# S5 loop of a hybrid S5 and Hyena encoder block: input matrices on VectorE, the skip's diagonal prepared once and added on GpSimd

## The chip, the core and the metric

The kernel runs on one core of a Trainium2 chip. The metric is the device time of one execution in microseconds (us), the median of several runs. Engines are named as in the profile: PE is TensorE (matmuls), PEld its weight loads, DVE is VectorE, ACT is ScalarE, POOL is GpSimd, SP issues DMAs.

## What is computed

One encoder block over 1024 positions of width 1024. Its first half merges two token mixers, a bidirectional S5 state-space model and an order-2 Hyena convolution; its second half is a SwiGLU channel mixer. The change concerns the S5 mixer alone:

```python
def _s5_scan(u, lam_re, lam_im, log_step, b_re, b_im, c_re, c_im, reverse):
    # abar = exp(lam * step), bb = (abar - 1) / lam * b, all complex
    ug = u.reshape(bsz, seq, S5_GROUPS, S5_GROUP)            # 32 groups of 16 channels
    bu_re = jnp.einsum('blgc,gpc->lbgp', ug, bb_re)          # 64 states a group
    bu_im = jnp.einsum('blgc,gpc->lbgp', ug, bb_im)
    # s[l] = abar * s[l-1] + bu[l], along the sequence or against it
    return (jnp.einsum('lbgp,gcp->blgc', s_re, c_re) - jnp.einsum('lbgp,gcp->blgc', s_im, c_im)).reshape(bsz, seq, D_S5)

def _s5_branch(u, ...):
    y = u * d                                                # the skip, d per channel
    for direction in range(2):
        y = y + _s5_scan(u, ..., reverse=(direction == 1))
    z = gelu(y)
    return z * sigmoid(z @ glu_w + glu_b)
```

## The kernel before

The kernel is written in a tile framework. The program names tiles and instructions; a scheduler puts each engine's instructions in a fixed order by its own estimate of times and adds the waits. So the order on an engine is not that of the source, and a change in one place can move rows elsewhere. Each engine works through its own list in order.

The S5 mixer (`emit_s5`) cuts the sequence into 128 blocks of 8 positions. In each block of 8 the effect of inputs on outputs is a small local kernel; from block to block the state is carried by a scan of 128 steps. A loop `for q in range(8)` (line 779) makes four channel groups a turn; below, "group" means one turn of this loop. The two directions lie in partitions 0 to 63 (`f`) and 64 to 127 (`b`). One turn does this:

- Output matrices: `ct`, `nct` are the transposed C and its negative; `cc0`, `cc1` are C times powers of abar, four products (line 800) and two sums (line 801) on VectorE.
- Input matrices: `Bw` is B times powers of abar (`eb`), by the helper `cmul` (lines 591 and 592: four products `wt`, two sums `bw`), on GpSimd. TensorE transposes them (`tt`, line 809), ScalarE copies them into `BT`.
- Local kernel: TensorE multiplies `cc` by B (`bz`) into `kp` (line 821); ScalarE copies it to SBUF as `Kt`, and its backward half at lag 0 as `kb` (lines 825, 826). VectorE adds the skip, `diag` times the column `dcol` of d (line 827), and writes the sum at lag 0 into `Kt` (line 828). `Kt` goes to DRAM (`klines`) and comes back as the Toeplitz blocks `D` (line 834).
- Phases and rotation: lines 841 to 852 make `cos` and `sin` (two VectorE instructions over the tile, four over its quarters, `sin`); `bu` (line 859) is the input times `BT` on TensorE; lines 863 to 865 rotate it into `xs` on VectorE.
- Scan on VectorE (line 871) into `S`, rotation back: `z` on VectorE (lines 876, 877, 879), the imaginary part on GpSimd into `beside` (the same three lines). ScalarE copies both into `M`.
- Output: `yp` on TensorE, `cc` times `M` (line 885) plus `D` times the input (line 887); ScalarE copies it, DMA stores it in `zS`.

The input's projection matmuls (`pj`, lines 144 to 146, three for one product since weights `wh`, `wl` and inputs are split in two parts) for Hyena and the gates don't depend on S5 and are put between the S5 matmuls by the scheduler. Their weights are split on ScalarE (`wh`) and GpSimd (`wl`, line 136). After the loop the GLU (`emit_glu`) reads `zS` back (`zf`, line 1267) and multiplies it by its weights (`gl`).

Of the kernel before, what the change touches and what calls it, by code (L numbers as in the profile page):

```python
# [7 lines left out]
F32 = mybir.dt.float32  # L8
# [3 lines left out]
ALU = mybir.AluOpType  # L12
# [4 lines left out]
P = 128  # L17
# [566 lines left out]
def cmul(E, pool, out, a, b, shape, tag, eng=None, conj=False):  # L584

    eng = eng or E.nc.vector
    for k, op in enumerate((ALU.add, ALU.subtract) if conj else (ALU.subtract, ALU.add)):
        t = [pool.tile(shape, F32, tag=f"{tag}{i}", name=f"{tag}{i}") for i in range(2)]
        pairs = ((a[0], b[0]), (a[1], b[1])) if k == 0 else ((a[1], b[0]), (a[0], b[1]))
        for i in range(2):  # L590
            eng.tensor_tensor(out=t[i], in0=pairs[i][0], in1=pairs[i][1], op=ALU.mult)
        eng.tensor_tensor(out=out[k], in0=t[0], in1=t[1], op=op)
# [151 lines left out]
def emit_s5(E, before):  # L744
# [3 lines left out]
    V, GP = nc.vector, nc.gpsimd  # L748
    f, b = slice(0, 64), slice(64, 128)
    with ExitStack() as ctx:  # L750
        op = ctx.enter_context(E.tc.tile_pool(name="s5k", bufs=1, reuse_waits="tile"))
# [6 lines left out]
        with E.tc.tile_pool(name="s5p", bufs=1, reuse_waits="tile") as pp:  # L758
            bball, r8, wh, wl, ec, eb = s5_params(E, op, pp, ps)
            before()  # L760
        sp = ctx.enter_context(E.tc.tile_pool(name="s5", bufs=1, reuse_waits="tile"))
        halfpi = op.tile([P, 1], F32, name="halfpi")
        V.memset(halfpi, float(np.pi / 2))
        dcol = op.tile([64, 8], F32, name="dcol")
        nc.sync.dma_start(out=dcol, in_=d["s5_d"][0].rearrange("(q r) -> r q", r=64))
        diag = op.tile([64, 16], F32, name="diag")
        V.tensor_copy(diag, E.ident[0:64, 0:16])
        for g in range(1, 4):
            V.tensor_tensor(out=diag, in0=diag, in1=E.ident[0:64, 16 * g:16 * g + 16], op=ALU.add)
        bz = [op.tile([P, 640], F32, name=f"bz{k}") for k in range(2)]  # L770
        W = P + 2
        xs = [op.tile([P, 4, W], F32, name=f"xs{k}") for k in range(2)]
# [5 lines left out]
        for q in range(8):  # L778
# [6 lines left out]
            e4 = lambda ap, n, m: ap[:, :, gs].rearrange("p t g -> p g t").unsqueeze(3).to_broadcast([P, 4, n, m])  # L785
            b4 = lambda ap, n, m: ap.unsqueeze(2).to_broadcast([P, 4, n, m])
# [14 lines left out]
                V.tensor_tensor(out=CC[k], in0=tmp[0], in1=tmp[1], op=sgn)  # L801
            Bb = [x[:, gs] for x in bball]
            Bw = [T(f"bw{i}", [P, 4, 8, 16]) for i in range(2)]
            cmul(E, sp, Bw, [b4(x, 8, 16) for x in Bb], [e4(x, 8, 16) for x in eb], [P, 4, 8, 16], "wt", GP)
            BT = []
            for i in range(2):
                pt = ps.tile([P, 4, P], F32, tag="tt", name="tt", bufs=2)
# [10 lines left out]
            kp = ps.tile([P, 9, 16], F32, tag="tt", name="kp", bufs=2)  # L818
# [4 lines left out]
            Kt = T("Kt", [P, 9, 16])  # L823
            kb = T("kb", [64, 16])
            nc.scalar.copy(Kt, kp)
            nc.scalar.copy(kb, kp[b, 0])
            V.scalar_tensor_tensor(out=kb, in0=diag, scalar=dcol[:, q:q + 1], in1=kb, op0=ALU.mult, op1=ALU.add)
            V.tensor_tensor(out=Kt[f, 0], in0=kp[f, 0], in1=kb, op=ALU.add)
            line = E.klines[gs].rearrange("g c x -> (g c) x")
            nc.sync.dma_start(out=line[:, 112:240], in_=Kt[f, 0:8].rearrange("p i c -> p (i c)"))  # L830
            nc.sync.dma_start(out=line[:, 0:112], in_=Kt[b, 2:9].rearrange("p i c -> p (i c)"))
# [12 lines left out]
            for g in range(4):  # L844
                V.scalar_tensor_tensor(out=ph[:, g], in0=j8[:, 0], scalar=col(wl, 4 * q + g), in1=ph[:, g],
                                       op0=ALU.mult, op1=ALU.subtract)
# [22 lines left out]
            for i in range(2):  # L869
                o, r, x = fl(S[i]), fl(rd), fl(xs[i])  # L870
                V.tensor_tensor_scan(out=o[:, 1:n], data0=r[:, 0:n - 1], data1=x[:, 0:n - 1], initial=0.0,
                                     op0=ALU.mult, op1=ALU.add)
# [911 lines left out]
def hybrid_block(tc, d):  # L1784
# [4 lines left out]
    with ExitStack() as top:  # L1789
# [18 lines left out]
        with ExitStack() as s0:  # L1808
            E.h0 = pool(s0, "h0")
            E.dft = pool(s1, "dft")  # L1810
            with ExitStack() as s2:
# [25 lines left out]
                for ct in range(4):  # L1837
                    emit_conv(E, ct)
                emit_ada(E, (2, 4, 3), *ada_rooms(E))
                emit_s5(E, lambda: [emit_u(E, ct) for ct in range(4)])  # L1840
                for ct in range(4, 12):
                    emit_conv(E, ct)
# [70 lines left out]
```

## Time and profile before

| | |
|---|---|
| median of 3 runs | 1740.43 us (1737.8 to 1741.24) |
| profiled execution | 1738.77 us, its span 1737.0 us |
| TensorE matmuls busy | 1552.6 us, 89% of the span |
| VectorE busy | 1326.7 us, 76% |
| ScalarE busy | 744.1 us, 43% |
| GpSimd busy | 641.1 us, 37% |

The S5 loop runs from about 393 to 630 us of the span. Shares over the whole span are averages over stages with different limits; what a change in one stage is worth is read from that stage, by what ended each engine's idle time there. The starts of one instruction in successive turns of a loop give the time of a turn, and the duration of the same instruction with and without work on another engine shows what the two do to each other.

### The profile page before, as it was taken

The numbers are of one execution on the slowest core, as the hardware profiler recorded it, in microseconds if no ns is written. First come the engines' busy times: TensorE is split into PE (matmuls) and PEld (weight loads), VectorE is DVE, ScalarE is ACT, GpSimd is POOL, SyncE is SP. The second block draws the span as 40 slices with busy tenths as digits, with TensorE's granted clock in tenths as the row PEclk, the third lists the DMA queues.
The fourth block names the chain that finished last, engine by engine and source line by source line (L and its number), as shares of the span: only waits on it lengthen the run. The fifth ranks groups of instructions, "written<-read, shape, count | busy, mean of one in ns | idle before, by whom it ended". The sixth has DMA issues, their size and how long they took to land. (4 is left out here: it accounts for less than half of the span.)

```text
span 1737.0 us, 22072 instructions
## 1 busy us (share of the span) xinstructions
PE 1552.6 (89%) x7598; PEld 1282.6 (74%) x7598; DVE 1326.7 (76%) x1927; ACT 744.1 (43%) x1366; POOL 641.1 (37%) x425
## 2 busy tenths in 40 slices
PE   6778889997678798998869999899999999999996
PEld 2666768785556686786757989688888888878884
DVE  6889798787898835788877656976676777579976
ACT  5846455443453444412223455533333333345445
POOL 3356564326575426768862121111111111012233
PEclk9998999998897999999989999899999999999998
DMA  9446643432122344864425853143323223499953
GB/s 329 123 141 185 181 132 113 153 100 82 50 71 67 88 112 156 285 233 155 122 85 184 279 181 97 49 135 113 104 92 103 92 97 99 146 380 319 328 190 126
DMA packets 244870, 263.81 MB, mean 152 GB/s; under 512 B 27672, under 2 KB 168816, under 8 KB 243317
## 3 DMA queue, kind: packets, MB, share of 16 engines
q1 hardware_dynamic: 244278, 259.99, 46.8%
q0 software_dynamic: 480, 2.42, 0.4%
q8 instruction: 60, 0.98, 0.2%
q14 instruction: 52, 0.43, 0.1%
HBM read 195.00 MB, written 67.34 MB: 151 GB/s over the span
## 5 line engine op out<-in xcount | busy, mean ns | idle before, releaser
L144 PE MATMUL pj<-hT,wh 128*128 128x512 f32 x480 | 195.6, 407 | 8.7 <-ACT cva L1184 8.0
L136 POOL TENSOR_TENSOR wl<-wf,wh 128x1024 fp32r<-128x1024 f32 (+1 forms) x56 | 127.9, 2285 | 200.3 <-ACT wh L135 150.1
L146 PE MATMUL pj<-hT,wl 128*128 128x512 f32 x480 | 194.8, 406 | 4.6 <-POOL wl L136 4.6
L136 POOL TENSOR_TENSOR wl<-wg,wh 128x1024 fp32r<-128x1024 f32 x22 | 55.4, 2521 | 345.3 <-ACT wh L135 345.3
L146 PE MATMUL gu<-h2T,op 128*128 128x512 f32 x440 | 172.8, 394 | 3.8 <-DVE op L136 3.8
L144 PE MATMUL gu<-h2T,op 128*128 128x512 f32 x440 | 171.4, 394 | 2.5 <-ACT op L135 2.5
L145 PE MATMUL gu<-h2T,op 128*128 128x512 f32 x440 | 173.1, 393 | 0.0
L135 ACT CAST op<-ws 128x512 fp32r<-128x512 f32 x88 | 54.4, 622 | 182.9 <-PE gu L146 111.1
L145 PE MATMUL dn<-dop 128*128 128x512 f32 x308 | 120.2, 390 | 0.3 <-POOL dop L136 0.3
L146 PE MATMUL dn<-dop 128*128 128x512 f32 x308 | 120.0, 390 | 0.0
L144 PEld LDWEIGHTS pj<-hT,wh 128*128 128x128 f32 x480 | 94.6, 197 | 28.3 <-ACT cva L1184 8.7
L144 PE MATMUL dn<-dop 128*128 128x512 f32 x308 | 112.3, 391 | 2.2 <-ACT dop L135 2.1
L146 PEld LDWEIGHTS pj<-hT,wl 128*128 128x128 f32 x480 | 94.3, 196 | 25.1 <-POOL wl L136 5.4
L145 PE MATMUL pj<-hT,wh 128*128 128x512 f32 x256 | 102.9, 402 | 0.0
L146 PEld LDWEIGHTS gu<-h2T,op 128*128 128x128 f32 x440 | 83.6, 190 | 22.4 <-DVE op L136 5.0
L144 PEld LDWEIGHTS gu<-h2T,op 128*128 128x128 f32 x440 | 83.5, 190 | 21.5 <-ACT op L135 3.2
L145 PEld LDWEIGHTS gu<-h2T,op 128*128 128x128 f32 x440 | 83.5, 190 | 17.0
L145 PE MATMUL pj<-lT,wh 128*128 128x512 f32 x224 | 91.1, 407 | 0.0
L136 POOL TENSOR_TENSOR dop<-bf,dop 128x512 fp32r<-128x512 f32 x17 | 31.4, 1852 | 128.7 <-ACT dop L135 112.6
L1535 DVE TENSOR_TENSOR ws<-wu 128x512 f32<-128x512 f32 x22 | 25.3, 1149 | 64.0 <-DMA wu<-in_ffn_w_gu_dram 64.0
L144 PE MATMUL wop<-woh,mT 128*128 128x256 f32 x256 | 73.1, 286 | 0.9 <-DVE tmp L1410 0.9
L135 ACT CAST wh<-wf 128x1024 fp32r<-128x1024 f32 (+1 forms) x56 | 50.0, 893 | 55.5 <-PE pj L145 24.6
(461 smaller groups left out, 4494.0 us busy)
## 6 DMA issues: line engine op xcount, KB each, us to landing
bf<-in_ffn_w_down_dram SPq DMA_DIRECT2D x105, 256.0 KB
wf<-in_w_in_dram SPq DMA_DIRECT2D x36, 512.0 KB
ada<-in_ada_w_dram SPq DMA_DIRECT2D x48, 256.0 KB
wg<-in_ffn_w_gu_dram SPq DMA_DIRECT2D x22, 512.0 KB
wu<-in_ffn_w_gu_dram SPq DMA_DIRECT2D x22, 512.0 KB
adS<-S SPq DMA_DIRECT2D x44, 256.0 KB
af<-adS SPq DMA_DIRECT2D x44, 256.0 KB
adA<-a SPq DMA_DIRECT2D x33, 256.0 KB
```

The costliest lines, as they stand in the source:

```text
L135: E.nc.scalar.copy(hi, src)
L136: (lo_eng or E.nc.vector).tensor_tensor(out=lo, in0=src, in1=bc(hi), op=ALU.subtract)
L144: E.nc.tensor.matmul(out=out, lhsT=lh, rhs=rh, start=first, stop=False, skip_group_check=shared)
L145: E.nc.tensor.matmul(out=out, lhsT=lh, rhs=rl, start=False, stop=False, skip_group_check=shared)
L146: E.nc.tensor.matmul(out=out, lhsT=ll, rhs=rh, start=False, stop=last, skip_group_check=shared)
L1535: V.tensor_tensor(out=s1, in0=u1, in1=u2, op=ALU.add)
```

## The change

The six instructions of `cmul` for `Bw` go from GpSimd to VectorE (48 in the loop). The diagonal matrices of the skip, `dd`, are made once ahead of the loop, by eight small VectorE instructions; inside it GpSimd adds `dd[:, q]` to `kb` and then `kb` to `Kt` at lag 0. VectorE no longer touches the local kernel, and line 828 no longer reads `kp` from PSUM, which GpSimd adds to from `Kt` instead.

```diff
--- before.py
+++ after.py
@@ -767,6 +767,9 @@
         V.tensor_copy(diag, E.ident[0:64, 0:16])
         for g in range(1, 4):
             V.tensor_tensor(out=diag, in0=diag, in1=E.ident[0:64, 16 * g:16 * g + 16], op=ALU.add)
+        dd = op.tile([64, 8, 16], F32, name="dd")
+        for q in range(8):
+            V.tensor_scalar(out=dd[:, q], in0=diag, scalar1=dcol[:, q:q + 1], scalar2=None, op0=ALU.mult)
         bz = [op.tile([P, 640], F32, name=f"bz{k}") for k in range(2)]
         W = P + 2
         xs = [op.tile([P, 4, W], F32, name=f"xs{k}") for k in range(2)]
@@ -801,7 +804,7 @@
                 V.tensor_tensor(out=CC[k], in0=tmp[0], in1=tmp[1], op=sgn)
             Bb = [x[:, gs] for x in bball]
             Bw = [T(f"bw{i}", [P, 4, 8, 16]) for i in range(2)]
-            cmul(E, sp, Bw, [b4(x, 8, 16) for x in Bb], [e4(x, 8, 16) for x in eb], [P, 4, 8, 16], "wt", GP)
+            cmul(E, sp, Bw, [b4(x, 8, 16) for x in Bb], [e4(x, 8, 16) for x in eb], [P, 4, 8, 16], "wt")
             BT = []
             for i in range(2):
                 pt = ps.tile([P, 4, P], F32, tag="tt", name="tt", bufs=2)
@@ -824,8 +827,8 @@
             kb = T("kb", [64, 16])
             nc.scalar.copy(Kt, kp)
             nc.scalar.copy(kb, kp[b, 0])
-            V.scalar_tensor_tensor(out=kb, in0=diag, scalar=dcol[:, q:q + 1], in1=kb, op0=ALU.mult, op1=ALU.add)
-            V.tensor_tensor(out=Kt[f, 0], in0=kp[f, 0], in1=kb, op=ALU.add)
+            GP.tensor_tensor(out=kb, in0=kb, in1=dd[:, q], op=ALU.add)
+            GP.tensor_tensor(out=Kt[f, 0], in0=Kt[f, 0], in1=kb, op=ALU.add)
             line = E.klines[gs].rearrange("g c x -> (g c) x")
             nc.sync.dma_start(out=line[:, 112:240], in_=Kt[f, 0:8].rearrange("p i c -> p (i c)"))
             nc.sync.dma_start(out=line[:, 0:112], in_=Kt[b, 2:9].rearrange("p i c -> p (i c)"))
```

The scheduler orders the whole program anew. Lines behind the new ones count three higher in the listings of the new kernel.

VectorE, between the first sum `cc0` of a group and the rotation of `bu`, in the third group, before (the number behind a tile's name is its buffer):

```order
L801 TENSOR_TENSOR cc0_3188<-rt0_3190,rt1_3191 128x576
L843 SCALAR_TENSOR_TENSOR ph_3425<-phk_3426,ph_3425 128x512
L800 TENSOR_TENSOR rt0_3195<-nct_3185,ec1_2486 128x576
L800 TENSOR_TENSOR rt1_3196<-nct_3185,ec0_2485 128x576
L845 SCALAR_TENSOR_TENSOR ph_3425<-j8_2291,s5keep_2529,ph_3425 128x128 x4
L801 TENSOR_TENSOR cc1_3189<-rt0_3195,rt1_3196 128x576
L863 TENSOR_TENSOR rt0_3297<-bu0_3279,cos_3260 128x512
L827 SCALAR_TENSOR_TENSOR kb_3240<-diag_2825,dcol_2823,kb_3240 64x16
L864 TENSOR_TENSOR rt1_3298<-bu1_3288,sin_3261 128x512
```

The same place in the fourth group, after:

```order
L804 TENSOR_TENSOR cc0_3364<-rt0_3366,rt1_3367 128x576
L591 TENSOR_TENSOR wt0_3550<-bb1_2512,eb0_2487 128x512
L591 TENSOR_TENSOR wt1_3551<-bb0_2511,eb1_2488 128x512
L845 TENSOR_SCALAR phk_3602<-ph_3601 128x512
L803 TENSOR_TENSOR rt0_3371<-nct_3361,ec1_2486 128x576
L803 TENSOR_TENSOR rt1_3372<-nct_3361,ec0_2485 128x576
L592 TENSOR_TENSOR bw1_3544<-wt0_3550,wt1_3551 128x512
L846 SCALAR_TENSOR_TENSOR ph_3601<-phk_3602,ph_3601 128x512
L804 TENSOR_TENSOR cc1_3365<-rt0_3371,rt1_3372 128x576
L591 TENSOR_TENSOR wt0_3712<-bb0_2511,eb0_2487 128x512
L591 TENSOR_TENSOR wt1_3713<-bb1_2512,eb1_2488 128x512
L848 SCALAR_TENSOR_TENSOR ph_3601<-j8_2291,s5keep_2529,ph_3601 128x128 x4
```

In the one, the local kernel's line 827 stands between the two uses of `bu`; in the other it is gone, and five instructions of `cmul` stand between `cc0` and the first use of `bu`, of the next group's input matrices and the one after.

GpSimd in the loop, from a weight split on, before:

```order
L136 TENSOR_TENSOR wl_5020<-wf_5017,wh_5019 128x1024
L876 TENSOR_TENSOR beside_2840<-S0_2973,sin_2927 128x512
L592 TENSOR_TENSOR bw0_3200<-wt0_3202,wt1_3203 128x512
L877 TENSOR_TENSOR beside_2840<-S1_2974,cos_2926 128x512
L591 TENSOR_TENSOR wt0_3207<-bb1_2512,eb0_2487 128x512
L591 TENSOR_TENSOR wt1_3208<-bb0_2511,eb1_2488 128x512
L879 TENSOR_TENSOR beside_2840<-beside_2840 128x512
L592 TENSOR_TENSOR bw1_3201<-wt0_3207,wt1_3208 128x512
L591 TENSOR_TENSOR wt0_3369<-bb0_2511,eb0_2487 128x512
```

and after, again from a weight split on:

```order
L136 TENSOR_TENSOR wl_5089<-wf_5086,wh_5088 128x1024
L830 TENSOR_TENSOR kb_3082<-kb_3082,dd_2830 64x16
L879 TENSOR_TENSOR beside_2849<-S0_3149,sin_3103 128x512
L831 TENSOR_TENSOR Kt_3081<-Kt_3081,kb_3082 64x16
L880 TENSOR_TENSOR beside_2849<-S1_3150,cos_3102 128x512
L882 TENSOR_TENSOR beside_2849<-beside_2849 128x512
L136 TENSOR_TENSOR wl_5149<-wf_5146,wh_5148 128x1024
L879 TENSOR_TENSOR beside_2849<-S0_3316,sin_3270 128x512
L830 TENSOR_TENSOR kb_3249<-kb_3249,dd_2830 64x16
```

The input matrices have left; the two adds of the local kernel stand among the products `beside` of the same group: in the second group the second add behind the first product, in the third (the last two rows) both behind it. That is so for one add or both in four of eight groups; in the others both adds stand ahead of the products.

On TensorE the order changes in which projection matmuls stand where. Behind the last `yp` and ahead of the first GLU matmul there are 162 of them before and 123 after; the loop, from its first transpose to its last `yp`, holds 413 before and 441 after. Before the loop's first transpose 11 more run after the change than before it. All or most of `bu` stands behind the last `kp` of its group in the fourth, the sixth and the eighth group after the change, and a part of it behind the first `kp` in the second. In the FFN some rows of VectorE, ScalarE and TensorE change places; nothing is added or removed there.

## Rows read from the trace of the kernel before

**Rows 1.** Busy time by stretch (start:end us, length), with granted TensorE clock.

```profile
core 0: us, PE busy (x) PEld busy (x) DVE busy (x) ACT busy (x) POOL busy (x), PEclk, DMA share, GB/s
392.90:630.20 237.30, 185.65 (x1070) 151.87 (x1071) 196.90 (x206) 100.76 (x217) 131.47 (x79) 0.86 0.26 71
630.20:673.00 42.80, 38.21 (x168) 30.95 (x167) 8.94 (x4) 22.59 (x23) 14.61 (x6) 1.00 0.55 151
```

**Rows 2.** What TensorE waited for, 392.9 to 630.2 us: total, times, longest.

```profile
PE kp L821 <- DVE cc L801: 33.6, 8, 7.2
PE yp L885 <- ACT M L881: 16.0, 7, 3.6
```

**Rows 3.** What VectorE waited for, the same stretch.

```profile
DVE kb L827 <- ACT kb L826: 23.4, 4, 6.2
```

**Rows 4.** Line 879 on VectorE: min/median/max ns, first and last start.

```profile
L879 DVE TENSOR_TENSOR z<-rt,rt x8: 673/1478/2765, 434.4 to 620.1; 128x512 f32<-128x512 f32 x8
```

**Rows 5.** Timeline of VectorE, last group: start us, us, instruction [idle before].

```profile
600.59 2.77 DVE L879 TENSOR_TENSOR z<-rt,rt 128x512 f32<-128x512 f32 x1
...
604.95 1.41 DVE L800 TENSOR_TENSOR rt<-ct,ec 128x576 f32<-128x576 f32 x2
...
617.33 1.67 DVE L877 TENSOR_TENSOR rt<-S,sin 128x512 f32<-128x512 f32 x1
...
620.11 0.67 DVE L879 TENSOR_TENSOR z<-rt,rt 128x512 f32<-128x512 f32 x1
```

**Rows 6.** Timeline of VectorE in an earlier group.

```profile
493.02 3.24 DVE L800 TENSOR_TENSOR rt<-ct,ec 128x576 f32<-128x576 f32 x2
...
498.10 3.05 DVE L800 TENSOR_TENSOR rt<-nct,ec 128x576 f32<-128x576 f32 x2
```

**Rows 7.** Timeline of GpSimd in the same stretch.

```profile
492.51 3.13 POOL L591 TENSOR_TENSOR wt<-bb,eb 128x512 f32<-128x512 f32 x2
```

**Rows 8.** Timeline of VectorE: a product of `cmul`, and the steps of a phase.

```profile
370.87 0.68 DVE L591 TENSOR_TENSOR bt<-braw,s5scr 128x512 f32<-128x512 f32 x1
...
444.62 0.41 DVE L842 TENSOR_SCALAR phk<-ph 128x512 f32<-128x512 f32 x1
...
445.63 0.68 DVE L843 SCALAR_TENSOR_TENSOR ph<-phk,ph 128x512 f32<-128x512 f32 x1
...
447.43 1.12 DVE L845 SCALAR_TENSOR_TENSOR ph<-j,s5keep,ph 128x128 f32<-128x128 f32 x4
```

**Rows 9.** Timeline of VectorE, first group.

```profile
390.31 0.41 DVE L842 TENSOR_SCALAR phk<-ph 128x512 f32<-128x512 f32 x1
...
414.90 0.76 DVE L801 TENSOR_TENSOR cc<-rt,rt 128x576 f32<-128x576 f32 x1
...
422.16 0.23 DVE L827 SCALAR_TENSOR_TENSOR kb<-diag,dcol,kb 64x16 f32<-64x16 f32 x1 [5.70 <-ACT kb L826]
```

**Rows 10.** Timeline of TensorE and VectorE at a wait for line 826.

```profile
477.78 0.66 PE L859 MATMUL bu<-U,BT 128*64 128x128 f32 x8
...
478.67 0.23 DVE L827 SCALAR_TENSOR_TENSOR kb<-diag,dcol,kb 64x16 f32<-64x16 f32 x1 [5.57 <-ACT kb L826]
...
478.82 0.67 DVE L864 TENSOR_TENSOR rt<-bu,sin 128x512 f32<-128x512 f32 x1
```

**Rows 11.** Timeline of TensorE: two projection matmuls, one behind the other.

```profile
480.83 0.39 PE L145 MATMUL pj<-lT,wh 128*128 128x512 f32 x1
...
481.06 0.39 PE L146 MATMUL pj<-hT,wl 128*128 128x512 f32 x1
```

**Rows 12.** Timeline of the DMA queue: line 1267 first and last, line 765.

```profile
631.37 4.32 SPq L1267 DMA_DIRECT2D zf<-zS  x6
...
653.66 1.52 SPq L1267 DMA_DIRECT2D zf<-zS  x3
...
353.01 2.17 SPq L765 DMA_DIRECT2D dcol<-in_s_d_dram  x1
```

**Rows 13.** Line 740 on GpSimd, small copies: min/median/max ns.

```profile
L740 POOL COPY s5keep<-s5scr x3: 212/215/537, 361.8 to 368.7; 128x32 f32<-128x32 f32 x3
```

## The prediction

> **What bounds the kernel now.** The change lies in the S5 loop of eight channel groups, so I read the busy time of that stretch first, then what each engine waited for in it, then the timeline of single groups.
>
> From the first matmul of the loop to its last TensorE is busy 185.65 of 237.30 us at a granted clock of 0.86, VectorE 196.90, GpSimd 131.47 [rows 1]. Right behind it the clock is 1.00 and TensorE hardly pauses [rows 1]. The time to win is therefore inside the loop, 51.65 us of TensorE's pauses at most, plus what the lower clock costs. TensorE's pauses are mainly waits for VectorE: 33.6 us before the local kernel's matmuls (`kp`, line 821) for the products `cc` (line 801), and 16.0 us before `yp` for `M`, which ScalarE copies from VectorE's `z` [rows 2]. VectorE itself waits 23.4 us in four groups for `kb`, ScalarE's copy of `kp` [rows 3]. So the loop is a circle: VectorE makes `cc`, TensorE makes `kp` and `bu`, VectorE goes on with `bu` to `z`, TensorE goes on with `z`.
>
> The beat of the circle is the start of `z` on VectorE: 434.4 us for the first, 600.59 for the seventh, 620.11 for the last [rows 4, 5]. That is (600.59 - 434.4) / 6 = 27.7 us a group for six groups, and 19.52 for the last.
>
> Why are they so different? In the last group GpSimd has no input matrices left to make, VectorE has no phase of a next group to make, and it never waits for `kb`. How much GpSimd's products matter is seen at line 800: two products take 1.41 us on VectorE in the last group [rows 5], but 3.24 and 3.05 us in an earlier one [rows 6], while GpSimd makes its own two products there in 3.13 us [rows 7]. The two engines take turns; (3.24 - 1.41) / 2 = 0.9 us is lost on VectorE for each such GpSimd instruction that meets it.
>
> **The change part by part.** The sum is made on the profiled execution (1738.77 us, span 1737.0, 1.77 us around it). That run lies 1.66 us, 0.1%, under the median of 1740.43 us; I take the difference that I find off the median.
>
> *1. Input matrices on VectorE.* 48 instructions (six a group) leave GpSimd. The same helper, the same shape, made on VectorE before the loop, takes 0.68 us [rows 8], so six cost 4.1 us a group. What a group costs without GpSimd's products I take from the last group, which is a measurement of just that: 19.52 us. It holds the remaining GpSimd work already, a weight split beside its first `z` (2.77 us against 0.67 us bare) and the `beside` products (1.67 us against 0.67 us in one instruction) [rows 5]. It lacks the phase of a next group, 0.41 + 0.68 + 1.12 = 2.2 us [rows 8]. Together 19.5 + 2.2 + 4.1 = 25.8 us, before waits, against 27.7 us with them.
>
> *2. The skip on GpSimd.* Lines 827 and 828 leave VectorE. Their work is small, 0.23 us for the first where nothing disturbs it [rows 10], so 0.2 us a group go: 25.6 us. The wait for `kb` goes too, but that is worth little by itself: at 478.67 us VectorE starts line 827 after 5.57 us of waiting, and the eight `bu` matmuls that its next instruction needs end on TensorE at 477.78 + 0.66 = 478.44 us [rows 10]. Without line 827, line 864 would have waited for `bu` until then. What counts is whether TensorE still puts `bu` behind `kp`. By the new order it does so in four of eight groups (all or most of it in the fourth, sixth and eighth, part of it in the second); but in the second, fourth and sixth VectorE now has three to five instructions of `cmul`, 2.0 to 3.4 us, to make between `cc` and `bu`, in the place of the wait. The four waits were 23.4 us, 5.70 of them in the first group [rows 3, 9], so 17.7 / 6 = 2.95 us per interval. I keep 0.4 us of it, between 0 and 2.95. An interval is then 26.0 us, and six save 6 x 1.7 = 10 us. Bounds: 25.0 us (a saving of 16; the products at 0.6, no wait) and 28.5 us (a loss of 5; the whole wait comes back).
>
> *3. The first group.* From the phase at 390.31 us to the end of the second `cc` at 415.66 VectorE takes 25.35 us [rows 9]. At the bare prices it has two phases (4.4), a sine product (0.7), and two sets of `cc` products at 1.41 + 0.76 (4.3): 9.4 us [rows 5, 8, 9]. Now come twelve products (8.2) and two meetings with weight splits of 2.1 us each, (2.77 - 0.67) [rows 5]: 21.8 us, 3.5 less. Of the wait of 5.70 us behind it [rows 9] I let the half go. Together 6 us; between 1 and 11.
>
> *4. The adds on GpSimd.* 16 small adds; small copies there take 0.21 to 0.54 us [rows 13], so 3.4 to 8.6 us in all on an engine that loses 48 instructions in the same stretch. The first of each pair waits for ScalarE's copy of `kb`; behind it stand the `beside` products or the next weight split, for which TensorE's `yp` and projections wait. GpSimd's idle time, 237.30 - 131.47 us before [rows 1], hides both; where it doesn't, it is the third rival.
>
> *5. The last group.* In the new order 3 projection matmuls stand between the last `yp` products, 19 in the order before. Two such start 0.23 us apart [rows 11], so 16 x 0.23 = 3.7 us. The last local kernel is also written earlier, ahead of the `beside` products instead of behind them. Against it stands that the eighth group's `bu` comes behind `kp` with nothing between, so that VectorE may wait there as it did not before. I take 2 us, between -3 and 4.
>
> *6. The tail.* After the last `yp` 123 projection matmuls stand in front of the GLU's, 162 before: 39 x 0.23 = 9 us, which now fill pauses of the loop. Against it stands the reload of S5's output: 32 transfers whose issue takes from 631.37 to 655.18 us [rows 12]. The remaining 123 x 0.23 = 28 us cover that with little to spare, so I give 1.5 us back: 7.5 us, between 3 and 9.
>
> *7. `dd`.* Eight VectorE instructions among the S5 parameters, on whose chain the loop begins. The like tile takes 0.23 us [rows 10]: 1.8 us. They need `dcol`, whose transfer is issued from 353.01 to 355.18 us [rows 12], about when VectorE would get to them, so it can also stand there for a moment, with all parameters behind it. I charge 2 us, between 0 and 4.5.
>
> Sum: -10 - 6 - 2 - 7.5 + 2 = -23.5 us. Later stages keep their work; a shuffle of some rows in the FFN I price at nothing, because TensorE runs on there through other rows.
>
> **The rivals.**
>
> *No gain in the loop.* VectorE gives back exactly what it wins, and `bu` takes the place of `kb`. For it: 19.5 + 2.2 + 4.1 - 0.2 + 2.95 = 28.6 us, which is no better than 27.7. Against it: the products stand where VectorE waited. With intervals of 27.7 us and nothing in the first group, the last group, the tail and `dd` are left: -2 - 7.5 + 2 = -7.5, so 1733 us. The Trainium skill, page Perfetto Trace Analysis, section Optimizing Scalar/DVE Operations, speaks for this rival: it warns that VectorE and GpSimd share a read port of SBUF, so that moving work between these two might not help. This trace agrees that they block each other (0.9 us an instruction, above); by that rule items 1 to 3 are worth nothing, and the sum is the -7.5.
>
> *Slower: the products stand ahead of `cc`.* In the new order up to five products lie between `z` and the second `cc`. TensorE's wait for `cc` [rows 2] then grows, `kp` and `bu` come later, and VectorE waits for `bu` longer than it did for `kb`. The other items are worth 13.5 us, so it decides from 13.5 / 6 = 2.3 us more per interval, 30.0 us. With a full wait of 6 us in every group, the longest of before [rows 3], an interval is 25.6 + 6 = 31.6 us: 6 x 3.9 - 13.5 = +10, so 1750 us.
>
> *GpSimd's queue.* In four groups the second of the adds, in two of them both, stand behind a `beside` product that needs the scan, so the local kernel and its reload come late and `yp` waits for `D`. Nothing waits for `D` now to speak of. At 4 us in each of four groups: -23.5 + 16 = -7.5, 1733 us.
>
> *More.* With fewer pauses the clock stays up and intervals fall to 24 us: 6 x 2 more, so -35.5, 1705 us.
>
> **How the numbers follow.** The forecast, 1707 to 1728 us around 1717, gets 0.50; no gain in the loop 0.20; slower 0.14; GpSimd's queue 0.08; more 0.08. The range runs from 1698 (into the last case) to 1740 us, which leaves out most of the slower case and a little of "more". 0.2%, 3.5 us, is about what a measurement of this kernel can tell from no change: most of the slower case lies above 1744, 0.12; between lie its rest and the upper part of "no gain", 0.10; faster is 0.78.
>
> **What would show it.** Right: starts of `z` some 26 us apart; line 800 at 0.7 to 0.8 us an instruction except beside `wl` and `beside`; little VectorE waiting, for `bu`; TensorE's wait for `cc` under 33.6 us; the first GLU matmul about 24 us earlier. Wrong: starts of `z` 28 us or more apart, with VectorE waiting for `bu` as long as it did for `kb`, or TensorE waiting for `D`.

## The result and the profile after

| | before | after |
|---|---|---|
| median | 1740.84 us (1737.8 to 1743.99, 4 runs) | 1694.97 us (1693.18 to 1695.76, 4 runs) |
| profiled execution, its span | 1738.77, 1737.0 us | 1695.38, 1693.6 us |
| first matmul of the loop | 393.01 us | 393.69 us |
| first start of `z` | 434.40 us | 421.11 us |
| mean of six intervals between starts of `z` | 27.70 us | 23.95 us |
| last interval | 19.52 us | 22.80 us |
| end of the last `yp` | 630.22 us | 594.98 us |
| first GLU matmul | 672.01 us | 623.84 us |

The ratio is 0.9738 (95% interval 0.9724 to 0.9751): 45.9 us less, where 23.5 were forecast. The sign and the place were right, the size was not: 1694.97 us lies 3 us under the low end of the range.

The busy time by stretch in the kernel after: the loop, what follows it up to the GLU, both together, and the six intervals. Columns as in [rows 1].

```profile
core 0: us, PE busy (x) PEld busy (x) DVE busy (x) ACT busy (x) POOL busy (x), PEclk, DMA share, GB/s
393.69:594.98 201.29, 178.79 (x1099) 148.57 (x1099) 182.83 (x237) 99.93 (x217) 72.27 (x50) 0.96 0.30 84
594.98:623.84 28.86, 28.34 (x124) 22.77 (x123) 7.36 (x4) 20.32 (x19) 11.16 (x5) 1.00 0.69 190
393.69:623.84 230.15, 207.13 (x1222) 171.34 (x1221) 190.19 (x241) 120.25 (x236) 83.43 (x54) 0.96 0.35 97
421.11:564.82 143.71, 126.78 (x790) 105.01 (x788) 138.12 (x179) 76.68 (x170) 53.94 (x37) 0.95 0.30 84
```

VectorE has 237 instructions in the loop instead of 206 and is nevertheless busy for 182.83 us instead of 196.90 [rows 1]. It now works through 138.12 of the 143.71 us of the six intervals; 0.93 us an interval are pauses. The granted clock of the loop is 0.96 of 2.4 GHz, 0.86 before; both are means over stretches at 2.4 GHz and stretches at 1.2 GHz.

The same two stretches of the kernel before, joined, and its six intervals (columns as above):

```profile
393.01:672.01 279.00, 222.87 (x1231) 181.96 (x1232) 205.73 (x210) 122.37 (x238) 145.70 (x84) 0.88 0.30 83
434.40:600.59 166.19, 127.39 (x740) 104.67 (x741) 146.39 (x157) 76.49 (x168) 95.40 (x57) 0.85 0.24 65
```

From the loop's first matmul to the GLU the time fell from 279.00 to 230.15 us. TensorE's busy time in it fell by 15.74 us at nearly the same number of matmuls (1231 and 1222 recorded), TensorE's pauses from 56.13 to 23.02 us.

TensorE's waits for `M` and `cc`, and VectorE's longest waits, in the loop after (us in total, times, longest):

```profile
PE yp L888 <- ACT M L884: 13.3, 7, 4.3
PE kp L824 <- DVE cc L804: 3.0, 3, 1.5
```

```profile
DVE rt L866 <- PE bu L862: 6.5, 2, 6.1
DVE bw L592 <- PE tt L812: 3.7, 2, 3.0
```

TensorE's wait for `cc`, 33.6 us [rows 2], is 3.0 us; VectorE's wait for `kb`, 23.4 us [rows 3], is gone, and `bu` takes 6.5 us in its place, nearly all of it in one wait of the last group. The wait of `yp` for `M` has hardly changed (16.0 and 13.3 us).

The groups of VectorE's instructions in the S5 stage (from 385 to 640 us), count, busy us, mean ns, before:

```profile
L800 DVE TENSOR_TENSOR rt<-ct,ec 128x576 f32<-128x576 f32 x16 | 25.8, 1649 | 0.0
L801 DVE TENSOR_TENSOR cc<-rt,rt 128x576 f32<-128x576 f32 x16 | 18.4, 1152 | 0.5
L877 DVE TENSOR_TENSOR rt<-S,sin 128x512 f32<-128x512 f32 x8 | 12.4, 1552 | 0.0
L863 DVE TENSOR_TENSOR rt<-bu,cos 128x512 f32<-128x512 f32 x16 | 11.0, 687 | 0.6
```

and after:

```profile
L591 DVE TENSOR_TENSOR wt<-bb,eb 128x512 f32<-128x512 f32 x32 | 22.7, 749 | 0.0
L592 DVE TENSOR_TENSOR bw<-wt,wt 128x512 f32<-128x512 f32 x16 | 15.6, 973 | 3.8 <-PE tt L812 3.7
L880 DVE TENSOR_TENSOR rt<-S,sin 128x512 f32<-128x512 f32 x8 | 12.5, 1566 | 0.0
L804 DVE TENSOR_TENSOR cc<-rt,rt 128x576 f32<-128x576 f32 x16 | 12.0, 752 | 0.3
L803 DVE TENSOR_TENSOR rt<-ct,ec 128x576 f32<-128x576 f32 x16 | 11.3, 748 | 0.0
L866 DVE TENSOR_TENSOR rt<-bu,cos 128x512 f32<-128x512 f32 x16 | 11.0, 687 | 6.7 <-PE bu L862 6.5
```

The products for `cc` fell from 1649 to 748 ns and their sums from 1152 to 752. The products of `S`, which meet GpSimd's `beside` in both kernels, stayed at 1.55 us. And the products of `bu` took 687 ns before and after: of the two inputs `bu` lies in PSUM, and in none of the twelve traces does one of these products in the loop take more than 694 ns.

### The profile page after: what moved, and what is told of

Read it like the earlier page. It is cut to its first block, busy times and chain, and to the rows that moved or that the text cites. A ratio compares the mean times of both kernels' runs of the same rounds, so it can differ in the third digit from the quotient of the medians.

```text
span 1693.6 us, 22059 instructions
## 1 busy us (share of the span) xinstructions
PE 1539.2 (91%) x7598; PEld 1272.2 (75%) x7598; DVE 1316.4 (78%) x1967; ACT 743.4 (44%) x1366; POOL 577.6 (34%) x393
## 5 line engine op out<-in xcount | busy, mean ns | idle before, releaser
L144 PE MATMUL pj<-hT,wh 128*128 128x512 f32 x480 | 193.5, 403 | 9.0 <-ACT cva L1187 8.3
L145 PE MATMUL pj<-hT,wh 128*128 128x512 f32 x256 | 101.1, 395 | 0.0
L144 PEld LDWEIGHTS gu<-h2T,op 128*128 128x128 f32 x440 | 83.5, 190 | 23.4 <-ACT op L135 3.2
L146 PEld LDWEIGHTS gu<-h2T,op 128*128 128x128 f32 x440 | 83.5, 190 | 22.5 <-DVE op L136 5.0
L145 PE MATMUL wop<-wol,mT 128*128 128x256 f32 x256 | 72.5, 283 | 0.0
```

Source lines behind the costliest of these rows:

```text
L144: E.nc.tensor.matmul(out=out, lhsT=lh, rhs=rh, start=first, stop=False, skip_group_check=shared)
L145: E.nc.tensor.matmul(out=out, lhsT=lh, rhs=rl, start=False, stop=False, skip_group_check=shared)
L146: E.nc.tensor.matmul(out=out, lhsT=ll, rhs=rh, start=False, stop=last, skip_group_check=shared)
```

## The experiments

The theory is the prediction's own, with a larger price: what counts is that GpSimd's instructions hold up VectorE, and 48 of them left. Against it stand the wait for `kb` (the skip), late input matrices (tt and `bu` wait for GpSimd's `Bw`), and VectorE's own load (if VectorE bounds the loop, its 48 new instructions cost what they take). A third stands beside these: with fewer products on GpSimd its other work, `beside` and the weight splits, comes sooner. The scheduler orders every version anew, and the number of projection matmuls that it leaves for the tail moves with it (29 to 159 in the versions below), so I compare the whole time, and the time from the loop's first matmul to the GLU.

| version | median, us | ratio to before (95%) | loop to GLU, us | TensorE busy in it | pauses in it |
|---|---|---|---|---|---|
| before | 1740.5 to 1741.0 | 1 | 279.00 | 222.87 | 56.13 |
| after | 1694.97 | 0.9738 (0.9724 to 0.9751) | 230.15 | 207.13 | 23.02 |
| input matrices only | 1698.05 | 0.9759 (0.9734 to 0.9785) | 231.91 | 210.10 | 21.81 |
| skip only | 1740.87 | 1.0009 (0.9997 to 1.0022) | 276.28 | 221.15 | 55.13 |
| inputs of the first turn only | 1695.48 | 0.9748 (0.9724 to 0.9771) | 230.42 | 208.84 | 21.58 |
| the same, 42 idle products on GpSimd | 1728.76 | 0.9934 (0.9916 to 0.9953) | 266.81 | 221.51 | 45.30 |
| half of the inputs on GpSimd | 1716.79 | 0.9861 (0.9846 to 0.9876) | 251.09 | 217.28 | 33.81 |
| `beside` on VectorE too | 1688.82 | 0.9695 (0.9680 to 0.9710) | 220.77 | 203.40 | 17.37 |
| weight splits on VectorE too | 1682.69 | 0.9654 (0.9637 to 0.9671) | 210.74 | 194.15 | 16.59 |
| both on VectorE too | 1660.98 | 0.9539 (0.9525 to 0.9553) | 193.23 | 187.70 | 5.53 |
| both, only the projections' splits | 1665.35 | 0.9559 (0.9539 to 0.9579) | 202.71 | 189.46 | 13.25 |
| both, inputs back on GpSimd | 1690.37 | 0.9708 (0.9669 to 0.9747) | 226.06 | 197.77 | 28.29 |

The last three columns are from one profiled execution each. That stretch holds 1220 to 1231 matmuls in the first eight rows and 1175 in the last four, where 45 more projection matmuls run ahead of the loop, so the last four compare with each other rather than with those above.

**Which part of the change.** The one half alone:

```diff
-            cmul(E, sp, Bw, [b4(x, 8, 16) for x in Bb], [e4(x, 8, 16) for x in eb], [P, 4, 8, 16], "wt", GP)
+            cmul(E, sp, Bw, [b4(x, 8, 16) for x in Bb], [e4(x, 8, 16) for x in eb], [P, 4, 8, 16], "wt")
```

> Only the input matrices go to VectorE; the skip stays as it was, with its wait for kb on VectorE. Theory (blocking): the 48 products on GpSimd cost VectorE up to 0.9 us each, and taking them off GpSimd is nearly the whole gain of 45.9 us, so 1697 to 1705 us, with intervals between starts of z of 24 to 25 us. Rival (the wait): VectorE's 23.4 us of waits for kb were the larger part, and they stay here: 1712 to 1725 us, intervals of 26 to 27 us.

It took 1698.05 us, 42.5 us under the 1740.54 of before in the same comparison, with intervals of 23.4 us, a little under the 24 to 25 that I expected. VectorE still waited for `kb`, but for 6.9 us instead of 23.4:

```profile
DVE kb L827 <- ACT kb L826: 6.9, 3, 3.2
```

So the wait shrank with line 827 still in its place. TensorE's own wait for `cc` is 3.4 us here instead of 33.6, so `kp` comes sooner.

The other half alone (with `dd` as in the change), the input matrices staying on GpSimd:

```diff
-            V.scalar_tensor_tensor(out=kb, in0=diag, scalar=dcol[:, q:q + 1], in1=kb, op0=ALU.mult, op1=ALU.add)
-            V.tensor_tensor(out=Kt[f, 0], in0=kp[f, 0], in1=kb, op=ALU.add)
+            GP.tensor_tensor(out=kb, in0=kb, in1=dd[:, q], op=ALU.add)
+            GP.tensor_tensor(out=Kt[f, 0], in0=Kt[f, 0], in1=kb, op=ALU.add)
```

> Only the skip is changed: dd made once, both adds on GpSimd; the input matrices stay on GpSimd. Blocking: the wait for kb on VectorE turns into a wait for bu, which ends at about the same time, so 1735 to 1743 us. The wait: VectorE goes on where it waited for kb, 1715 to 1728 us, intervals of 25 to 26 us.

No change: 1740.87 us. VectorE's largest wait in its loop shows why:

```profile
DVE rt L867 <- PE bu L862: 22.1, 4, 8.0
```

23.4 us of waiting for `kb` [rows 3] became 22.1 us of waiting for `bu`, four times again. TensorE makes `kp` and `bu` one behind the other, and both stand behind `cc`. Nearly the whole gain (42.5 of 45.9 us) is the input matrices'; the rival of the wait falls.

**The price of a product on either engine.** Here the input matrices are made in the first turn only, on VectorE:

```diff
-            Bw = [T(f"bw{i}", [P, 4, 8, 16]) for i in range(2)]
-            cmul(E, sp, Bw, [b4(x, 8, 16) for x in Bb], [e4(x, 8, 16) for x in eb], [P, 4, 8, 16], "wt")
+            if q == 0:
+                cmul(E, sp, Bw, [b4(x, 8, 16) for x in Bb], [e4(x, 8, 16) for x in eb], [P, 4, 8, 16], "wt")
```

(`Bw` is allocated ahead of the loop.) A second version adds products on GpSimd that nothing waits for:

```diff
+            else:
+                for k in range(2):
+                    t = [sp.tile([P, 4, 8, 16], F32, tag=f"wt{i}", name=f"it{i}") for i in range(2)]
+                    for i in range(2):
+                        GP.tensor_tensor(out=t[i], in0=b4(Bb[i ^ k], 8, 16), in1=e4(eb[i], 8, 16), op=ALU.mult)
+                    GP.tensor_tensor(out=t[0], in0=t[0], in1=t[1], op=(ALU.subtract, ALU.add)[k])
```

> The changed kernel, with the input matrices made in the first turn only (the other seven turns use those, so 42 products are left out). VectorE bounds the loop: 42 x 0.6 = 25 us less than the changed kernel, 1668 to 1675 us, intervals of 20 to 21 us. If instead the waits between VectorE and TensorE bound it (kp, bu, yp), the products filled pauses, and little goes: 1685 to 1694 us, intervals of 23 us or more.

> As the run with the input matrices of the first turn only, with 42 like products on GpSimd whose output nobody reads (turns 1 to 7). Blocking alone: each costs VectorE 0.9 us though nobody waits for it, 30 to 40 us more than the run without them, intervals up by 5 us. Rival (late products): what cost time in the kernel before was that Bw came late from GpSimd and with it tt, BT and bu; here nobody waits for them, so within 8 us of the run without them.

The loop without 42 products, then the loop with them idle on GpSimd, by stretch (the loop, and the tail up to the GLU):

```profile
396.87:585.44 188.57, 170.76 (x1062) 141.09 (x1063) 158.34 (x196) 98.91 (x215) 66.50 (x49) 0.96 0.31 88
585.44:627.29 41.85, 38.08 (x160) 30.43 (x160) 8.71 (x4) 21.61 (x21) 14.14 (x5) 0.96 0.53 143
```

```profile
395.24:625.01 229.77, 187.00 (x1079) 152.05 (x1079) 201.27 (x195) 100.07 (x217) 128.31 (x92) 0.90 0.26 73
```

VectorE has the same instructions in both, yet it is busy for 158.34 us in the one and for 201.27 in the other: 42.93 / 42 = 1.02 us of VectorE for each idle product of GpSimd, on average. In the kernel after, where VectorE makes the 42 itself, it is busy for 182.83 us: 24.49 / 42 = 0.58 us each. So a product costs VectorE more when GpSimd makes it. In the end the 42 idle products cost 1728.76 - 1695.48 = 33.3 us, 0.79 us each, though nothing waits for their results. Late input matrices are thus not what the kernel before mainly suffered from; in its own trace, too, no wait of TensorE up to the GLU is put down to GpSimd's `bw`. What the remaining difference between this version and the one of before (12 us) is made of, I have not taken apart.

The first of the two runs contradicts my main expectation: 24.5 us less work on VectorE in the loop, and the time is that of the kernel after (1695.48 and 1694.97 us). It lies 1.5 us above the range of the second case, that the products filled pauses, though the interval is shorter than that case had it (21.55 us, not 23 or more). The loop is 12.7 us shorter, but 36 projection matmuls more stand in the tail, which is 13.0 us longer. And VectorE now waits for `bu`:

```profile
DVE rt L868 <- PE bu L863: 10.3, 5, 5.3
DVE rt L867 <- PE bu L863: 8.7, 2, 4.8
```

TensorE's pauses up to the GLU are 21.58 us without the 42 products and 23.02 us with them. VectorE's products lengthen the intervals between starts of `z` (from 21.55 to 23.95 us), but not the time to the GLU: TensorE has the same work to do up to there, and a shorter loop leaves more of the projections for the tail. What counts at the end is how long TensorE pauses, and at which clock it works. The products on VectorE stand where they make TensorE pause no more; those on GpSimd make it pause 24 us longer (45.30 us), and at a clock of 0.90 instead of 0.96 in the loop it is busy for 12.7 us more.

**More or less of the same.** The imaginary half of the input matrices back on GpSimd (24 instructions; the helper takes an engine for each half here):

```diff
-            cmul(E, sp, Bw, [b4(x, 8, 16) for x in Bb], [e4(x, 8, 16) for x in eb], [P, 4, 8, 16], "wt")
+            cmul(E, sp, Bw, [b4(x, 8, 16) for x in Bb], [e4(x, 8, 16) for x in eb], [P, 4, 8, 16], "wt", (V, GP))
```

> The changed kernel with the imaginary half of the input matrices back on GpSimd (24 of the 48 instructions). If each product on GpSimd has its price (1.0 us of VectorE, of which the run with 42 idle ones showed 33 us in the end, 0.8 each), 18 to 22 us over the changed kernel: 1712 to 1718 us. If GpSimd hurts only once it is too full to finish in time, this much still fits: 1694 to 1702 us.

1716.79 us, 21.8 us over the kernel after, 0.91 us each. The cost grows with the number, and 24 of them already cost about as much each as all 48 (45.9 us together with the skip, 0.96 each). Fewer than 24 I did not run.

If so, what is still on GpSimd should cost as well. Three versions of the kernel after move the `beside` products, the weight splits, and both:

```diff
-            for i, sgn, eng in ((0, ALU.subtract, V), (1, ALU.add, GP)):
+            for i, sgn, eng in ((0, ALU.subtract, V), (1, ALU.add, V)):
...
-    split(E, f, h, l, nc.gpsimd)
+    split(E, f, h, l, nc.vector)
```

> The changed kernel with the three products for the imaginary part of the state (24 in all) on VectorE too. By the price of a product (1.02 us of VectorE when on GpSimd, 0.58 when on VectorE) VectorE's busy time in the loop falls by 24 x 0.44 = 10 us, but TensorE has only 23 us of pauses left between the loop's start and the GLU and a loop with 24 us less of VectorE work was no faster: 1688 to 1697 us. Rival: the imaginary part is now made behind z instead of beside it, so that yp waits some 2 us more for M in each turn: 1700 to 1712 us.

> The changed kernel with the low parts wl of the projections' and the GLU's weights on VectorE (11 of them in the loop, 2.8 us each on GpSimd now). A split beside VectorE work costs VectorE 2.1 us on GpSimd and by its 1024 columns about 1.2 us on VectorE, so VectorE's busy time falls by some 10 us: 1686 to 1697 us. Rival: VectorE comes to a split late, and the projection matmuls that fill TensorE's pauses wait for wl: 1702 to 1715 us.

> Both of these at once: in the loop GpSimd is left with the two small adds alone. If the two engines' meetings still cost anything in the end, this is the fastest: 1680 to 1692 us, with VectorE instructions of 128x512 at 0.7 us or less. If TensorE's waits bound the loop now, 1690 to 1700 us; if VectorE's own queue becomes the bound, 1702 us and over.

Together they are worth 34 us more: 1660.98 us, 79.7 us (4.6%) less than before. This beats both kernels. Apart they are worth 6.2 us, within my range, and 12.3 us, which is 3 us under the low end of mine. VectorE's busy time in the loop fell by 5.7 and 6.0 us, where I had 10 for each. The two together give more than the sum of the two, and my 1680 to 1692 us was too cautious; that TensorE's waits or VectorE's own queue would bound the loop then was wrong. With `beside` alone on VectorE I had feared that `yp` waits longer for `M`; in that run it waits for 3.9 us where it was 13.3, and `z` takes 0.68 us where it was 1.42:

```profile
PE yp L888 <- ACT M L884: 3.9, 5, 1.8
```

The loop of the version with both, and some of its groups on VectorE:

```profile
389.15:567.98 178.83, 178.83 (x1138) 149.63 (x1138) 167.15 (x262) 103.30 (x220) 8.35 (x16) 1.00 0.37 102
```

```profile
L136 DVE TENSOR_TENSOR wl<-wf,wh 128x1024 fp32r<-128x1024 f32 x16 | 20.5, 1279 | 4.5 <-ACT wh L135 4.5
L803 DVE TENSOR_TENSOR rt<-ct,ec 128x576 f32<-128x576 f32 x16 | 11.3, 747 | 0.0
L866 DVE TENSOR_TENSOR rt<-bu,cos 128x512 f32<-128x512 f32 x16 | 11.0, 689 | 0.7
L880 DVE TENSOR_TENSOR rt<-S,sin 128x512 f32<-128x512 f32 x8 | 5.5, 686 | 0.0
L882 DVE TENSOR_TENSOR z<-rt,rt 128x512 f32<-128x512 f32 x8 | 5.4, 679 | 0.0
```

The profile shows no pause of TensorE in the loop, at a granted clock of 1.00, and VectorE with 262 instructions is busy for 167.15 us, against 196.90 for 206 before. `z`, 1.4 us in the kernel after, takes 0.68. With only the small adds left on GpSimd, the last four of these forms stand at their lowest price. (Part of the 34 us lies ahead of the loop and in the tail: 45 more projection matmuls run before the loop's first matmul, which still comes 4.5 us earlier.)

Two variations of this version. In the first, only the projections' splits are on VectorE and the later ones stay on GpSimd (an engine handed to the loader of weights, `eng=E.nc.vector` in `proj` alone). In the second, the input matrices go back to GpSimd, with the `"wt", GP` of before.

> As the run with the imaginary part and all weight splits on VectorE, but only the projections' splits of that go to VectorE; the later ones (GLU, branches, merge) stay on GpSimd, since in that run the part behind the first GLU matmul took 1077 us against 1070 in the changed kernel. Theory: the loop keeps its whole gain (TensorE without pauses), and the later part loses its extra: 1654 to 1660 us. Rival: the later part's 7 us come from the order of loads and not from the splits: 1660 to 1664 us.

> The imaginary part and all weight splits on VectorE, and the input matrices back on GpSimd: does it matter which work meets VectorE there, or only how much? By the price of a product on GpSimd (0.8 to 1.0 us each in the end, 33 to 46 us for 42 to 48) it is 1694 to 1707 us, as far behind the version with all on VectorE as the kernel before was behind the changed one. If GpSimd, now with nothing else, makes the input matrices where VectorE waits anyway, or has room to spread them: 1660 to 1680 us.

The first took 1665.35 us, 4.4 us more than the version with both and above both of my cases. Its profiled execution was its longest (1674.43 us), and in that one TensorE waited once for the reloaded Toeplitz blocks, which the other version's loop doesn't show:

```profile
PE yp L890 <- DMA D<-klines: 7.8, 1, 7.8
```

So the price of the later part isn't read from this run. The second took 1690.37 us, 29.4 us over the version with all on VectorE, 0.61 us for each of 48. That is under my 0.8 to 1.0, and 3.6 us under the range that I drew from it: here the products cost less in the end, but far from nothing.

This run also answers what the idle products leave open. There `beside` and the weight splits wait their turn in GpSimd's list and could have come late by the added products. Here GpSimd has nothing but the input matrices and the two small adds, and VectorE is still busy for 180.83 us in the loop, 13.7 us more than in the version with both, with 40 instructions fewer. TensorE's long waits in the loop are for `M` and `cc`, none for `bw` or `D`:

```profile
PE yp L888 <- ACT M L884: 12.7, 6, 2.9
PE kp L824 <- DVE cc L804: 8.2, 3, 4.4
```

## Why the prediction was wrong, and where it was right

Sum of the differences of the two profiles (393.01 to 393.69 and so on, from the first table): +0.7 up to the loop, -14.0 to the first `z`, -22.5 in six intervals, +3.3 in the last interval, -2.7 from the last `z` to the end of `yp`, -12.9 in the tail, and +4.8 behind the first GLU matmul (1064.99 and 1069.76 us). Together -43.4 us, which are the two spans; the medians are 45.9 apart.

*Steps 1 and 2, forecast -10, measured -22.5.* This is the step that failed, and in it the sentence that what a group costs without GpSimd's products is "a measurement of just that: 19.52 us". With the phase, and without the skip's lines, I made it 21.5 us of VectorE's work an interval. The version without the products has 116.68 us of it in its six intervals, 19.4 each:

```profile
424.31:553.59 129.28, 115.73 (x752) 96.09 (x748) 116.68 (x145) 74.16 (x166) 46.43 (x35) 0.97 0.30 86
```

That is 2.1 us an interval. One group stood for all, and I gave it no range. It was not the meetings that I named, the split on `z` and `beside` on a product [rows 5], that made it dear: in the version without the products they recur, at 2.88 and 1.68 us in the group around 465 us. But the 19.52 us hold 0.48 us in which VectorE paused, and line 827 at 1.25 us beside a `beside` product, for which I took off 0.2:

```profile
600.59:620.11 19.52, 16.64 (x106) 13.86 (x105) 19.04 (x19) 4.69 (x10) 8.50 (x5) 0.91 0.22 70
```

```profile
618.93 1.25 DVE L827 SCALAR_TENSOR_TENSOR kb<-diag,dcol,kb 64x16 f32<-64x16 f32 x1
```

That is some 1.5 of the 2.1 us; the rest I have not taken apart. A product I took at its duration, 0.68 us [rows 8], where starts follow each other faster than ends; in the timeline after, instructions of this size are 0.60 us apart, and the runs above give 0.58 for a product:

```profile
497.00 0.68 DVE L882 TENSOR_TENSOR z<-rt,rt 128x512 f32<-128x512 f32 x1
497.60 0.68 DVE L855 SCALAR_TENSOR_TENSOR sin<-ph,phk 128x512 f32<-128x512 f32 x1
498.20 1.42 DVE L803 TENSOR_TENSOR rt<-ct,ec 128x576 f32<-128x576 f32 x2
```

For six products that is 0.6 us an interval. The waits were 0.9 instead of 0.4 us, 0.5 the other way. 26.0 - 2.1 - 0.6 + 0.5 = 23.8, against 23.95 measured. A second error lies under the sum: I added up intervals and tail as if TensorE's work were fixed to places, and charged the products to the path in full. The run without them shows that they cost nothing up to the GLU. 48 meetings at the 0.9 us read from [rows 6] are 43 us, close to the 45.9 measured; I used that price to explain and not in the sum, and the sum by it would have needed what only that run shows, that the products are free on VectorE.

*Step 2, the skip.* Right: the wait for `kb` is worth nothing by itself, since `bu` ends at the same time. The run with the skip alone shows the exchange, 23.4 us for 22.1.

*Step 3, the first group, forecast -6, measured -14.0* from the loop's first matmul to the first `z`, near my bound of 11 but over it. From the phase at 391.87 us (390.31 before, [rows 9]) to the end of the second `cc` at 408.02 it is 16.2 us where I had 21.8, with ten of the twelve products in it: both pairs of products for `cc` stand at their bare 1.42 us, and the split that I let meet VectorE twice meets it once, at 392.20. The wait of 5.70 us behind it, of which I had let the half go, is gone whole: from the end of the second `cc` to `z` it was 18.7 us, and is 13.1.

```profile
392.20 2.87 DVE L592 TENSOR_TENSOR bw<-wt,wt 128x512 f32<-128x512 f32 x1
...
401.18 1.42 DVE L803 TENSOR_TENSOR rt<-ct,ec 128x576 f32<-128x576 f32 x2
...
407.26 0.76 DVE L804 TENSOR_TENSOR cc<-rt,rt 128x576 f32<-128x576 f32 x1
```

*Step 4, the adds on GpSimd.* Nothing is seen of a cost: TensorE never waits for `D` in the loop after.

*Step 5, the last group, forecast -2, measured +0.5* (+3.3 to `z`, -2.7 behind it). The loss that I named came, VectorE waiting for `bu` with nothing between it and `kp`:

```profile
564.82 1.75 DVE L882 TENSOR_TENSOR z<-rt,rt 128x512 f32<-128x512 f32 x1
...
577.91 0.69 DVE L866 TENSOR_TENSOR rt<-bu,cos 128x512 f32<-128x512 f32 x1 [6.14 <-PE bu L862]
...
587.62 1.60 DVE L882 TENSOR_TENSOR z<-rt,rt 128x512 f32<-128x512 f32 x1
```

*Step 6, the tail, forecast -7.5, measured -12.9.* The 39 fewer matmuls were right. What I missed stood in the tail of before, of which I had said that TensorE hardly pauses there: it is busy for 38.21 of 42.80 us [rows 1], and waited for the weight splits:

```profile
PE pj L146 <- POOL wl L136: 4.6, 2, 2.5
```

After, this is 0.5 us. And the reload of S5's output, for which I gave 1.5 us back, cost nothing: TensorE is busy for 28.34 of 28.86 us there.

*Step 7, `dd`.* 2 us forecast, 0.7 measured up to the loop's first matmul, within its bounds; 11 more projection matmuls stand in the same stretch.

*The FFN, "priced at nothing".* The part behind the first GLU matmul is 4.8 us longer in the profile after. Of this 2.0 us are one wait of TensorE for `g` at the FFN's start; most of the rest lies in the last 190 us, where I found no single wait. In the other versions that make the same there that part takes between 1064.8 and 1072.8 us, so a difference of this size is seen between orders, and I do not read it as the change's.

*The rivals.* "No gain in the loop" put VectorE's waits back in full; measured, 0.9 us an interval are left. With it falls, for this kernel, the warning of the Trainium skill (page Perfetto Trace Analysis, section Optimizing Scalar/DVE Operations) that moving work between the two engines might not help. They do block each other, but the blocked time (1.02 us) is more than the instruction's own (0.58 us). "Slower" needed TensorE's wait for `cc` to grow; it fell from 33.6 to 3.0 us. "GpSimd's queue" needed a wait for `D`, which isn't there. "More" had the right interval, 24 us, at a chance of 0.08, and partly for the wrong reason: the clock did stay up, but the interval is VectorE's work, 23.0 of 23.95 us, and that doesn't hang on TensorE's clock. What the clock gives is seen in TensorE's own busy time: at the 1222 matmuls of after, the mean of before (222.87 / 1231) would make 221.2 us; it is 207.13. So, as an estimate that takes the mix of matmuls as the same, some 14 of the 48.9 us between the loop's start and the GLU go with TensorE's higher clock (0.96 instead of 0.88 there); 33.1 are fewer pauses, and the rest is a few matmuls that run earlier.

## What to carry to other kernels

In these runs work that was handed to GpSimd was not off VectorE's path while both read SBUF: price such an instruction at what it takes from VectorE (here 1.02 us for a 128x512 product that VectorE makes in 0.58), count how many there are, and look for the forms on VectorE whose mean stands far over their lowest duration. A wait that two neighbours in a queue share (`kb`, then `bu`) was not won by removing one of them. A stage cost taken from a single turn of a loop needs a range of its own; and where a scheduler has filler for TensorE, a change is worth what it takes off TensorE's pauses, and gives to its clock, up to the point where the filler is used up, not what it takes off a turn.

## What the runs showed of the chip

GpSimd's products take 1.4 to 1.6 us each in the version with idle ones (by the profile, whose spans of GpSimd are rough), and VectorE loses 1.02 us by each on average, some 0.7 of their time, though no instruction of VectorE waits for their results:

```profile
L813 POOL TENSOR_TENSOR it<-bb,eb 128x512 f32<-128x512 f32 x28 | 39.0, 1411 | 4.6 <-DVE bw L592 4.1
L814 POOL TENSOR_TENSOR it<-it,it 128x512 f32<-128x512 f32 x14 | 21.9, 1562 | 0.5
```

VectorE's products with one input in PSUM were not held up. `rt<-bu,cos` has a mean of 687 ns before, 687 after and 689 where GpSimd has only the small adds, while `rt<-ct,ec`, with both inputs in SBUF, goes from 1649 over 748 to 747. The means of `bu` alone say little, since in the trace of before only 3 of its 32 products overlap an instruction of GpSimd. But where they meet they are not slowed: in the run with the skip alone two of them start inside one sum of GpSimd and take their usual time.

```profile
536.81 1.69 POOL L592 TENSOR_TENSOR bw<-wt,wt 128x512 f32<-128x512 f32 x1 [3.37 <-PE tt L812]
537.37 0.69 DVE L866 TENSOR_TENSOR rt<-bu,cos 128x512 f32<-128x512 f32 x1
537.97 0.68 DVE L867 TENSOR_TENSOR rt<-bu,sin 128x512 f32<-128x512 f32 x1
```

The Trainium skill (page SBUF — State Buffer, section SBUF: two separate sides) says that the pair of ports which the two engines share is locked for a whole instruction, and that a VectorE instruction with two SBUF inputs is among those that need it. These rows agree.

That a whole loop comes to run without a pause of TensorE in the profile, by giving VectorE 56 instructions more, I had not expected of an engine that was busy for 83% of it.
